# Both ConvFFN products of a two-layer encoder by Strassen's seven block products, in two phases with the activation's rows going through DRAM

## The chip, the cores and the metric

The kernel runs on one core of a Trainium2 chip. A core has TensorE (matrix products, out of SBUF into PSUM), VectorE, ScalarE, GpSimd (called Pool or POOL in the rows) and queues that start DMA transfers, here all by SyncE (SP). The metric is the device time of one execution in microseconds.

## The reference

The input x has 1024 positions of width 1024. Two layers follow each other; the first has a forgetting attention, the second a differential attention whose keys and values come from the first layer's end. After its attention each layer has a ConvFFN, which is what the change is about:

```python
def _conv_ffn(x, w_in, conv_w, conv_b, w_out):
    s = x.shape[1]
    u = x @ w_in                                   # 1024 -> 2 * 2816
    up = jnp.pad(u, ((0, 0), (CONV_WIDTH - 1, 0), (0, 0)))
    u = sum(conv_w[j] * up[:, j:j + s] for j in range(CONV_WIDTH)) + conv_b
    g, val = u[..., :D_FF], u[..., D_FF:]
    return (jax.nn.silu(g) * val) @ w_out          # 2816 -> 1024

x = _layer_norm(DN_ALPHA * x + mixer(x), ...)
x = _layer_norm(DN_ALPHA * x + _conv_ffn(x, ...), ...)
```

All values are float32.

## The kernel before

A float32 product is made of three products in a reduced format: each operand is split into a high part (a cast on ScalarE) and a low part (operand minus high part, a subtraction on VectorE or Pool, `split_w`, L173), and `mm3` (L186 to L197) sums high·high, high·low and low·high in PSUM. A matmul has a 128x128 weight block and 512 columns of the other operand.

x stands transposed in SBUF, as `xh` and `xl` for two halves of the positions. `x_from` (L235) makes it from a tile of 128 positions by eight transposes (`tps`), a cast and a subtraction for each half of the width.

`ffn` runs over 22 hidden tiles. `hidden(i)` loads the two weight tiles of a gate and a value tile, splits them, and makes `u` for all 1024 positions: 2 halves x 2 x 8 x 3 = 96 matmuls. Then come the convolution (one pass of ScalarE, L363, and two steps of VectorE, L365, for each half), Silu and the gate (L369), and the split into `hh` and `hl`. The activation stays in SBUF. `down` takes two hidden tiles at a time, 8 position tiles x 2 column halves x 2 x 3 = 96 matmuls into `dn`, and VectorE adds each result to `Y` (L398, L400). The down products of one pair of hidden tiles stand between the up products of the next. The last four hidden tiles are summed in `down_last`, where each position tile is normalised as its sum is done, and in layer 0 `tail_a` turns it into x again and starts the value projection (`vp`) of the next layer.

The start of `ffn` overlaps the attention's output projection: `op.tile(NT - 2)` and `steps` are its last two tiles of positions (`op` in the rows), and tiles that are done are turned into x between them. In the second layer the same function runs with other pools.

The order of each engine's instructions is set when the program is built, by a scheduler that starts from the order of the code and from priorities. At run time each engine takes its own queue in order, and waits where an operand isn't ready.

## Time and profile before

| what | value |
|---|---|
| median of 3 runs | 2674.91 us (2670.71 to 2676.68) |
| the profiled execution's own time | 2674.87 us |
| its span | 2673.1 us |
| mean granted clock of TensorE | 0.991 |
| TensorE / VectorE / ScalarE / Pool busy | 98% / 55% / 34% / 28% |
| DMA | 291.12 MB, mean 109 GB/s |

The span is the time from the first to the last instruction that the profile shows. A busy share counts matmuls as they overlap: a matmul row lasts about 0.39 us while the next one has begun 0.23 us after it. "PEclk" is the clock that the throttle granted, as a share of full speed. In rows, `out<-in` are the program's names; "idle before" is the time the engine stood still ahead of the instruction, with what ended it.

### The profile page before, as it was taken

How to read it: one execution, taken by the hardware profiler on the slowest of the kernel's cores; microseconds unless marked ns; L12 is line 12 of the kernel's file. 1: busy time of each engine (PE TensorE's matmuls, PEld its weight loads, DVE VectorE, ACT ScalarE, POOL GpSimd, SP SyncE). 2: the span in 40 equal slices, each digit the busy share in tenths (PEclk: the TensorE clock that was granted, in tenths of full speed). 3: DMA queues.
4: the chain of work that ended last, by engine and by line, in shares of the span. 5: the costliest groups of instructions: out<-in, count | busy, mean ns of one | idle time of the engine just before them, and what ended most of it. 6: DMA issues, size and time to landing. Idle time of an engine off the chain costs nothing. (4 is left out here: it accounts for less than half of the span.)

```text
span 2673.1 us, 35354 instructions
## 1 busy us (share of the span) xinstructions
PE 2619.5 (98%) x13576; PEld 2234.6 (84%) x13576; DVE 1457.0 (55%) x2742; ACT 917.7 (34%) x1544; POOL 760.8 (28%) x756
## 2 busy tenths in 40 slices
PE   8999999999999999999999999999999999999997
PEld 7989898777888888888888898988788888888886
DVE  5656656755444444444558685777544444444436
ACT  3544545523222222222235454553332222222221
POOL 3433334431111111111332545464411111111124
PEclk9999999999999999999999999989999999999999
DMA  7565646353111111111165546472521111111111
GB/s 251 170 191 163 209 147 192 127 191 122 48 48 48 48 49 54 48 48 48 56 199 165 174 125 205 129 237 76 204 92 50 53 48 48 48 48 48 48 40 63
DMA packets 136553, 291.12 MB, mean 109 GB/s; under 512 B 12464, under 2 KB 66736, under 8 KB 135360
## 3 DMA queue, kind: packets, MB, share of 16 engines
q1 hardware_dynamic: 136384, 288.86, 33.9%
q8 instruction: 107, 1.75, 0.3%
q14 instruction: 62, 0.51, 0.1%
HBM read 213.25 MB, written 75.56 MB: 108 GB/s over the span
## 5 line engine op out<-in xcount | busy, mean ns | idle before, releaser
L191 PE MATMUL u<-xh,whi 128*128 128x512 f32 x1408 | 547.9, 390 | 2.1 <-ACT xh L243 2.0
L191 PE MATMUL u<-xl,whi 128*128 128x512 f32 x1408 | 548.7, 390 | 0.1
L191 PE MATMUL u<-xh,wlo 128*128 128x512 f32 x1408 | 548.2, 389 | 0.0
L173 DVE TENSOR_TENSOR wlo<-raw,whi 128x1024 fp32r<-128x1024 f32 (+1 forms) x92 | 136.3, 1481 | 519.5 <-ACT whi L165 519.5
L191 PEld LDWEIGHTS u<-xh,whi 128*128 128x128 f32 x1408 | 264.0, 188 | 57.9 <-ACT xh L243 3.1
L191 PEld LDWEIGHTS u<-xl,whi 128*128 128x128 f32 x1408 | 264.3, 188 | 56.0 <-DVE xl L244 1.0
L191 PEld LDWEIGHTS u<-xh,wlo 128*128 128x128 f32 x1408 | 264.3, 188 | 54.8
L173 POOL TENSOR_TENSOR hl<-t,hh 128x1024 fp32r<-128x1024 f32 x42 | 100.7, 2397 | 641.6 <-ACT hh L165 641.6
L400 DVE TENSOR_TENSOR y<-y,dn 128x512 f32<-128x512 f32 x256 | 174.2, 685 | 173.7 <-PE dn L191 173.7
L191 PE MATMUL dn<-w2hi,hl 128*128 128x512 f32 x640 | 249.7, 390 | 0.0
L191 PE MATMUL dn<-w2lo,hh 128*128 128x512 f32 x640 | 249.7, 390 | 0.0
L191 PE MATMUL dn<-w2hi,hh 128*128 128x512 f32 x640 | 249.4, 390 | 0.0
L365 DVE SCALAR_TENSOR_TENSOR t<-u,cw,t 128x1023 f32<-128x1023 f32 (+1 forms) x176 | 224.9, 1278 | 40.6 <-ACT t L363 38.1
L173 POOL TENSOR_TENSOR w2lo<-raw,w2hi 128x1024 fp32r<-128x1024 f32 x40 | 96.1, 2402 | 479.3 <-ACT w2hi L165 448.6
L165 ACT CAST whi<-raw 128x1024 fp32r<-128x1024 f32 (+1 forms) x100 | 104.0, 1041 | 326.0 <-PE u L191 283.2
L191 PE MATMUL pj<-xh,whi 128*128 128x512 f32 x496 | 197.6, 398 | 2.0 <-DVE hl L645 1.9
L191 PE MATMUL pj<-xh,wlo 128*128 128x512 f32 x496 | 197.4, 398 | 0.0
L191 PE MATMUL pj<-xl,whi 128*128 128x512 f32 x496 | 197.1, 397 | 0.0
L501 DVE TENSOR_TENSOR tl<-tp,th 128x512 fp32r<-128x512 f32 (+1 forms) x240 | 149.9, 633 | 65.1 <-ACT th L500 60.2
L165 ACT CAST w2hi<-raw 128x1024 fp32r<-128x1024 f32 x40 | 42.0, 1051 | 384.7 <-PE dn L191 267.1
L500 ACT CAST th<-tp 128x512 fp32r<-128x512 f32 (+1 forms) x240 | 127.9, 543 | 119.5 <-PE tp L496 73.4
L684 POOL TENSOR_SCALAR pt<-pt,rr 128x128 f32<-128x128 f32 (+7 forms) x128 | 96.6, 761 | 221.7 <-DVE rr L683 179.9
(198 smaller groups left out, 5435.0 us busy)
## 6 DMA issues: line engine op xcount, KB each, us to landing
raw<-in_w_dram SPq DMA_DIRECT2D x132, 512.0 KB, 3.6
raw<-in_aqk_dram SPq DMA_DIRECT2D x16, 512.0 KB, 4.7
vd<-vt SPq DMA_DIRECT2D x32, 256.0 KB, 2.8
qd<-hl SPq DMA_DIRECT2D x32, 256.0 KB, 3.6
kd<-hl SPq DMA_DIRECT2D x32, 256.0 KB, 4.2
vv<-vd SPq DMA_DIRECT2D x16, 512.0 KB, 5.5
q<-qd SPq DMA_DIRECT2D x16, 512.0 KB, 4.6
ka<-kd SPq DMA_DIRECT2D x16, 512.0 KB, 6.1
```

What stands on the lines that cost most here:

```text
L165: nc.scalar.copy(out, in_)
L173: e.tensor_tensor(out, a, b, ALU.subtract)
L191: nc.tensor.matmul(ps, a, b, start=first and i == 0, stop=last and i == n - 1)
L365: nc.vector.scalar_tensor_tensor(t[:, j:], u[:, :S - j], cw[:, 2 - j, c:c + 1], t[:, j:], ALU.mult, ALU.add)
L400: nc.vector.tensor_tensor(Y[t][:, cc], Y[t][:, cc], o, ALU.add)
L500: nc.scalar.copy(th[:, :n], tp[:, :n])
L501: nc.vector.tensor_tensor(tl[:, :n], tp[:, :n], f32(th[:, :n]), ALU.subtract)
L684: nc.gpsimd.tensor_scalar(pt, pt, rr, 1.0, ALU.mult, ALU.mult)
```

## The change

The up product of a hidden pair and the down product are each cut into 2 x 2 blocks, and seven products of sums of blocks take the place of eight products of blocks.

Phase 1 (`hidden`, `w_parts`): the four weight blocks of a gate and a value tile (A11 to A22) give four sums S1 to S4; x gives four sums T1 to T4 and is kept as blocks B11, B21, B22. Seven products of 12 matmuls make the four results, three of which are summed in the PSUM bank `a`; ScalarE copies them into `ug` and `uv` and VectorE adds the others. Convolution and gate are as before. The gated row goes to DRAM (`h_d`); for each pair of hidden tiles Pool makes a sum of two halves (`s1_d`) and a difference of two weight halves (`t1_d`), which go to DRAM as well. The sums of x are made by `x_lo`, `x_hi` and `late`; those of three of the four position pairs take a way through DRAM (`xr_d`), as the pools have no room for them at first.

Phase 2: for each of seven products, eleven turns. A turn loads a pair of blocks of 128x512 from DRAM (`pair`), sums them where the product wants it, splits them together (`parted`: a ScalarE cast and a VectorE subtraction of 128x1024, into one of seven `opj` buffers) and runs 12 matmuls into four banks. Position tiles 4 to 7 are normalised during the seventh product, and tiles 0 to 3 after it.

The diff, cut to its core:

```diff
+        def x_lo(p, y, tags="TT"):
+
+            cs = slice(p * P, (p + 1) * P)
+            lows[p] = turned(y, tags)
...
+        def late(p, r, b22):
+
+            cs = slice(p * P, (p + 1) * P)
+            for h, src in (("T34", r), ("B22", b22)):
+                hi, lo = (w[..., cs] for w in X[h])
+                nc.scalar.copy(hi, src)
+                nc.vector.tensor_tensor(lo, src, f32(hi), ALU.subtract)
+
+        def x_hi(p, second, bounce):
+
+            cs = slice(p * P, (p + 1) * P)
+            (b11, b21), (b12, b22) = lows.pop(p), second
+            r, q = ((tmp if bounce else fp).tile([P, 2, 4, P], F32, name="xr", tag=tag, bufs=1 if bounce else 2)
+                    for tag in (("xr", "xq") if bounce else ("ug", "uv")))
+            nc.scalar.copy(r[:, 0], b12)
+            nc.vector.tensor_tensor(q[:, 0], b22, r[:, 0], ALU.subtract)
+            nc.vector.tensor_tensor(r[:, 0], r[:, 0], b11, ALU.subtract)
+            nc.vector.tensor_tensor(r[:, 1], b22, r[:, 0], ALU.subtract)
+            nc.vector.tensor_tensor(q[:, 1], b21, r[:, 1], ALU.subtract)
+            nc.scalar.copy(T12[0][..., cs], r)
+            nc.vector.tensor_tensor(T12[1][..., cs], r, f32(T12[0][..., cs]), ALU.subtract)
+            if bounce:
+                keep = tmp.tile([P, 512], F32, name="xb", tag="xb")
+                nc.scalar.copy(keep, b22.rearrange("p k s -> p (k s)"))
+                nc.sync.dma_start(out=xr_d[p][:, 0:2, :], in_=q.rearrange("p a k s -> p a (k s)"))
+                nc.sync.dma_start(out=xr_d[p][:, 2, :], in_=keep)
+            else:
+                late(p, q, b22)
...
+        x_lo(0, y[0])
+        x_hi(0, turned(y[1], "SS"), True)
         steps = op.tile(NT - 1)
-        for t in (4, 5):
-            plain(take(steps, 6))
-            x_from(Y[t], t)
+        plain(take(steps, 8))
+        x_lo(1, y[2])
+        y = [load_y(t) for t in (5, 2, 3)]
+        x_hi(1, turned(y[0], "SS"), True)
         plain(steps)
-        x_from(op.of(NT - 2), NT - 2, "TD")
...
+        x_lo(2, y[1])
+        x_hi(2, turned(op.of(NT - 2), "SS"), True)
+        x_lo(3, y[2], "SS")
...
+            split("A11", a11, "whi")
+            split("A12", a12, "wlo")
+            yield ops
+            s1 = both("S1", a21, a22, ALU.add)
+            s2 = both("S2", s1, a11, ALU.subtract)
+            split("S2", s2, "ws")
+            yield ops
+            split("S1", s1, "ws")
+            yield ops
+            split("S3", both("S3", a11, a21, ALU.subtract), "ws")
+            yield ops
+            split("S4", both("S4", a12, s2, ALU.subtract), "whi")
+            yield ops
+            split("A22", a22, "wlo")
+            yield ops
+
+        def product(ps, w, x, first=False):
...
+        def hidden(i, ops):
+
+            a = bank("S", "ua")
+            product(a, ops["A11"], X["B11"], first=True)
+            b = bank("D", "ub")
+            product(b, ops["A12"], X["B21"], first=True)
+            yield
+            ug = fp.tile([P, S], F32, name="ug", tag="ug", bufs=2)
+            uv = fp.tile([P, S], F32, name="uv", tag="uv", bufs=2)
+            with urgent():
+                nc.scalar.copy(ug[:, 0:512], a)
+                nc.vector.tensor_tensor(ug[:, 0:512], ug[:, 0:512], b, ALU.add)
+            product(a, ops["S2"], X["T2"])
+            with urgent():
+                nc.scalar.copy(ug[:, 512:S], a)
+            yield
+            c = bank("S", "uc")
+            product(c, ops["S1"], X["T1"], first=True)
+            with urgent():
+                nc.scalar.copy(uv[:, 512:S], c)
+            yield
+            product(a, ops["S3"], X["T3"])
+            with urgent():
+                nc.vector.tensor_tensor(uv[:, 512:S], uv[:, 512:S], a, ALU.add)
+            yield
+            product(c, ops["S4"], X["B22"])
+            with urgent():
+                nc.vector.tensor_tensor(ug[:, 512:S], ug[:, 512:S], c, ALU.add)
+            yield
+            product(a, ops["A22"], X["T4"])
+            with urgent():
+                nc.scalar.copy(uv[:, 0:512], a)
...
+                t = fp.tile([P, S], F32, name="tv" if half else "tg", tag="tv" if half else "tg", bufs=2 if half else 3)
+                nc.scalar.activation(t, u, AF.Identity, bias=cb[:, k:k + 1], scale=cw[:, 2, k:k + 1])
...
-            hi = fp.tile([P, S], F32R, name="hh", tag="hh", bufs=4)
-            lo = fp.tile([P, S], F32R, name="hl", tag="hl", bufs=4)
-            round_to("act", hi, ts[0])
-            sub("dve" if i == NH - 1 else "gps", lo, ts[0], f32(hi))
-            return hi, lo
...
+            nc.sync.dma_start(out=h_d[i], in_=ts[0])
+            made.append(ts[0])
+            if i % 2:
+                s1, m = made.pop(0), i // 2
+                nc.gpsimd.tensor_tensor(s1[:, 512:S], s1[:, 512:S], made.pop(0)[:, 512:S], ALU.add)
+                nc.sync.dma_start(out=s1_d[m], in_=s1[:, 512:S])
+                w = wpool.tile([P, D], F32, name="raw", tag="raw", bufs=2)
+                nc.sync.dma_start(out=w, in_=A["w2"][layer, 2 * m])
+                nc.gpsimd.tensor_tensor(w[:, 512:D], w[:, 512:D], w[:, 0:512], ALU.subtract)
+                nc.sync.dma_start(out=t1_d[m], in_=w[:, 512:D])
+            yield
...
+        parts = [w_parts(0), w_parts(1)]
+        todo = [hidden(i, next(g)) for i, g in enumerate(parts)]
+        for g in todo:
+            next(g)
+        y7 = turned(op.of(NT - 1), "TT")
+        fp = rest()
...
-        for n, c in enumerate(chunks):
-            hs = [hidden(c[0])]
-            if prev:
-                down(*prev)
-            hs += [hidden(i) for i in c[1:]]
-            prev = (c, hs, n == 0)
...
+        x_hi(3, y7, False)
+        for p in range(3):
+            r = fp.tile([P, 2, 4, P], F32, name="xr2", tag="ug", bufs=2)
+            b22 = fp.tile([P, 4, P], F32, name="xb2", tag="sr", bufs=3)
+            nc.sync.dma_start(out=r.rearrange("p a k s -> p a (k s)"), in_=xr_d[p][:, 0:2, :])
+            nc.sync.dma_start(out=b22.rearrange("p k s -> p (k s)"), in_=xr_d[p][:, 2, :])
+            late(p, r, b22)
+        plain(parts[0])
+        for i in range(NH):
+            g = todo[i]
+            if i >= 2:
+                next(g)
+            nxt = parts[i + 1] if i + 1 < len(parts) else None
+            if nxt is None and i + 1 < NH:
+                parts.append(w_parts(i + 1))
+                nxt = parts[-1]
+                todo.append(hidden(i + 1, next(nxt)))
+            for _ in range(6):
+                if next(g, 0) == 0:
+                    break
+                if nxt:
+                    next(nxt, None)
+            if nxt:
+                plain(nxt)
...
+        def pair(m, a, b):
+            tag = ("raw", "whi", "wlo", "whi", "wlo", "raw", "whi", "wlo")[ring[0] % 8]
+            ring[0] += 1
+            r = wpool.tile([P, 2, 512], F32, name="pr", tag=tag, bufs=2 if tag == "raw" else 3)
+            nc.sync.dma_start(out=r[:, 0], in_=src[a](m))
+            nc.sync.dma_start(out=r[:, 1], in_=src[b](m))
+            return r
...
+        def parted(*rs):
+            o = fp.tile([P, 2, 1088], F32R, name="opj", tag="opj", bufs=7)
+            if len(rs) == 1:
+                nc.scalar.copy(o[:, :, 0:512], rs[0])
+                nc.vector.tensor_tensor(o[:, :, 512:1024], rs[0], f32(o[:, :, 0:512]), ALU.subtract)
...
+        def turn(ps, o, m, first=False):
+            for t in range(4):
+                times(ps[t], o, t, first and m == 0, m == NM - 1)
...
+        As = [bank("S", "dna") for t in range(4)]
+        for m in range(NM):
+            turn(As, parted(pair(m, "A11", "B11")), m, first=True)
+        for t in range(4):
...
+            r5, r6 = pair(m, "S1", "T1"), pair(m, "A11", "B22")
+            nc.vector.tensor_tensor(s2[:, m], r5[:, 0], r6[:, 0], ALU.subtract)
+            nc.vector.tensor_tensor(t2[:, m], r6[:, 1], r5[:, 1], ALU.subtract)
+            turn(As, parted(s2[:, m], t2[:, m]), m)
+            turn(Cs, parted(r5), m, first=True)
...
+        def last(m):
+            r = pair(m, "A12", "B22")
+            nc.vector.tensor_tensor(r[:, 0], r[:, 0], s2[:, m], ALU.subtract)
+            return parted(r)
+
+        for t in range(4):
+            to_y(t + 4, lo_, As[t], True)
+            layer_norm(Y[t + 4], g_bc, b_bc, out(t + 4))
+        for m in range(NM - 4):
+            turn(Cs, last(m), m)
+            if m >= 2 and m < 6:
+                tail(m + 2, Y[m + 2], fp)
+        os = [last(m) for m in range(NM - 4, NM)]
+        for t in range(4):
+            for m, o in enumerate(os):
+                times(Cs[t], o, t, False, m == 3)
+
+            def add(h, t=t):
+                if h:
+                    to_y(t, hi_, Cs[t], False)
+
+            layer_norm(Y[t], g_bc, b_bc, out(t), t < 3, add)
+            tail(t, Y[t], fp)
...
-        if t == NT - 1:
-            plain(b_v(0, wv0, lambda: 0.0, range(0, 6)))
-            x_from(*pend.pop(0))
...
+        if t >= 4:
+            x_from(y, t, "SS")
+            if t == 6:
+                wv0.extend(b_v_weights(0))
+            return
...
+        if t == 3:
+            plain(b_v(0, wv0, lambda: 0.0, f, range(4, NT)))
+            x_from(*pend.pop(0), "TD")
```

Three places of the built order, each queue in its own order. First TensorE at the start of layer 0's ConvFFN, before: `tps` are the transposes of `x_from`, `yw` the last tile but one, `u` the first up product.

```order
L240 MATMUL tps<-ident_r,y_7195 128x128 [waits DMAHW3_49,DVE_49]
L240 MATMUL tps<-ident_r,y_7195 128x128 x3
L240 MATMUL tps<-ident_r,yw 128x128 x2
L191 MATMUL u<-xh_7198,whi 128x512 [waits Activation_49]
L191 MATMUL u<-xh_7198,whi 128x512
L240 MATMUL tps<-ident_r,y_7195 128x128 [waits DVE_49]
```

The first up matmuls stand between the transposes, and more transposes follow. The same place now, behind the A11 and A12 products of the first two hidden tiles: `yw` is the last tile, `ws` S2, `t12h` and `t12l` the parts of T2.

```order
L355 MATMUL tps<-ident_r,yw 128x128 [waits DVE_49,PE_49]
L355 MATMUL tps<-ident_r,yw 128x128 x3
L192 MATMUL ua<-t12h,ws 128x512 [waits Activation_49]
L192 MATMUL ua<-t12l,ws 128x512 [waits DVE_49]
L192 MATMUL ua<-t12h,ws 128x512 [waits DVE_49]
L192 MATMUL ua<-t12h,ws 128x512
L192 MATMUL ua<-t12l,ws 128x512
```

The S2·T2 product stands right behind the last tile's transposes; `ua<-b1h,whi` of the second hidden tile, with a wait for ScalarE, comes behind its 12 matmuls. On VectorE at the same place, now (the add that reads the last output matmul, L299, stands 20 rows further up; L373 is `late`, L425 and L420 are the sums and splits of `w_parts`):

```order
L373 TENSOR_TENSOR t34l<-xr_7634,t34h 128x8x128 [waits DMAHW4_49,DMAHW5_49,DMAHW0_49,Activation_49]
L373 TENSOR_TENSOR t34l<-xr,t34h 128x8x128 [waits Activation_49]
L373 TENSOR_TENSOR b22l<-xb_7635,b22h 128x4x128 [waits DMAHW6_49,Activation_49]
L373 TENSOR_TENSOR b22l<-xb_7643,b22h 128x4x128 [waits DMAHW7_49,Activation_49]
L373 TENSOR_TENSOR b22l<-xb_7651,b22h 128x4x128 [waits DMAHW0_49,Activation_49]
L425 TENSOR_TENSOR sr<-raw 128x512 [waits DVE_49]
L373 TENSOR_TENSOR t34l<-xr_7642,t34h 128x8x128 [waits DMAHW1_49,Activation_49]
L425 TENSOR_TENSOR sr<-sr,raw 128x512 [waits DVE_49]
L425 TENSOR_TENSOR sr<-raw 128x512
L373 TENSOR_TENSOR t34l<-xr_7650,t34h 128x8x128 [waits DMAHW2_49,Activation_49]
L459 TENSOR_TENSOR ug<-ug,ub 128x512 [waits Activation_49]
L420 TENSOR_TENSOR ws<-sr,ws 128x512 [waits Activation_49] x3
```

The low parts of T3, T4 and B22 stand ahead of the S2 low part (`ws<-sr,ws`), for which the product above waits. Second, VectorE in the first hidden tiles of layer 0, before, where the convolution of one tile (`t<-u`) meets the down products of two others:

```order
L173 TENSOR_TENSOR wlo<-raw,whi 128x1024 [waits DMAHW3_49,PE_49,Activation_49]
L398 SCALAR_TENSOR_TENSOR y_7192<-y_7192,dn 128x512 [waits PE_49]
L365 SCALAR_TENSOR_TENSOR t<-u,cw,t 128x1023 [waits Activation_49]
L398 SCALAR_TENSOR_TENSOR y_7192<-y_7192,dn 128x512 [waits PE_49]
L398 SCALAR_TENSOR_TENSOR y_7193<-y_7193,dn 128x512 [waits PE_49]
L365 SCALAR_TENSOR_TENSOR t<-u,cw,t 128x1022 [waits DVE_49]
```

The adds to `y` stand between the steps of a convolution. VectorE at the switch from phase 1 to phase 2 of layer 0, now:

```order
L471 TENSOR_TENSOR uv<-uv,ua 128x512 [waits PE_49,Activation_49]
L475 TENSOR_TENSOR ug<-ug,uc 128x512 [waits PE_49]
L486 SCALAR_TENSOR_TENSOR tg<-ug,cw,tg 128x1023 [waits DMAHW7_49,Activation_49]
L486 SCALAR_TENSOR_TENSOR tg<-ug,cw,tg 128x1022 [waits DVE_49]
L486 SCALAR_TENSOR_TENSOR tv<-uv,cw,tv 128x1023 [waits Activation_49]
L486 SCALAR_TENSOR_TENSOR tv<-uv,cw,tv 128x1022 [waits DVE_49]
L490 TENSOR_TENSOR tg<-tg,tv 128x1024 [waits DVE_49,Activation_49]
L576 TENSOR_TENSOR opj<-pr,opj 128x2x512 [waits DMAHW0_49,DMAHW1_49,PE_49,Activation_49]
L576 TENSOR_TENSOR opj<-pr,opj 128x2x512 [waits DMAHW3_49,DMAHW4_49,DMAHW2_49,Activation_49]
L576 TENSOR_TENSOR opj<-pr,opj 128x2x512 [waits DMAHW3_49,DMAHW5_49,DMAHW1_49,Activation_49]
```

All of the last hidden tile's convolution and gate stand ahead of the first split of phase 2 (`opj`). Third, TensorE at the end of layer 0's ConvFFN, before, from the last down matmuls:

```order
L191 MATMUL dn<-whi,hh 128x512
L191 MATMUL dn<-wlo,hh 128x512
L191 MATMUL dn<-whi,hl 128x512
L191 MATMUL vp<-whi,xh_11475 128x256 [waits Activation_49]
L191 MATMUL vp<-wlo,xh_11475 128x256
L191 MATMUL vp<-whi,xl_11476 128x256
```

The value projection `vp` follows the down product at once; the transposes of the last tiles stand between its later groups. The same place now (`y_10742` and `y_10743` are position tiles 2 and 3; those of tiles 0 and 1, which wait for Pool, stand right ahead):

```order
L245 MATMUL tps<-ident_r,y_10742 128x128 [waits DVE_49]
L245 MATMUL tps<-ident_r,y_10742 128x128 x3
L245 MATMUL tps<-ident_r,y_10743 128x128 [waits DVE_49]
L245 MATMUL tps<-ident_r,y_10743 128x128 x3
L192 MATMUL vp<-whi,x_12060 128x256 [waits DVE_49]
L192 MATMUL vp<-wlo,x_12060 128x256
```

The transposes of the tiles 0 to 3 stand ahead of the first `vp`.

## Rows read from the trace of the kernel before

**Rows 1.** The page: busy time by engine; then tenths busy of VectorE and granted clock by slice.

```profile
PE 2619.5 (98%) x13576; PEld 2234.6 (84%) x13576; DVE 1457.0 (55%) x2742; ACT 917.7 (34%) x1544; POOL 760.8 (28%) x756
...
DVE  5656656755444444444558685777544444444436
...
PEclk9999999999999999999999999989999999999999
```

**Rows 2.** Windows of 100 us in each ConvFFN: length, busy us (instructions) by engine, granted clock, DMA.

```profile
800.00:900.00 100.00, 100.00 (x443) 82.81 (x442) 45.39 (x49) 21.29 (x20) 13.63 (x6) 1.00 0.14 42
...
2100.00:2200.00 100.00, 100.00 (x442) 82.55 (x441) 43.13 (x41) 26.91 (x26) 14.38 (x6) 1.00 0.18 54
```

**Rows 3.** Groups by line and shape: busy us, mean ns of one, idle before, releaser.

```profile
L191 PE MATMUL u<-xh,whi 128*128 128x512 f32 x1408 | 547.9, 390 | 2.1 <-ACT xh L243 2.0
...
L400 DVE TENSOR_TENSOR y<-y,dn 128x512 f32<-128x512 f32 x256 | 174.2, 685 | 173.7 <-PE dn L191 173.7
...
L173 DVE TENSOR_TENSOR wlo<-raw,whi 128x1024 fp32r<-128x1024 f32 x90 | 135.1, 1501 | 517.8 <-ACT whi L165 517.8
...
L173 POOL TENSOR_TENSOR wlo<-raw,whi 128x1024 fp32r<-128x1024 f32 x47 | 113.8, 2423 | 27.9 <-ACT whi L165 25.8
...
L365 DVE SCALAR_TENSOR_TENSOR t<-u,cw,t 128x1023 f32<-128x1023 f32 x88 | 112.3, 1276 | 38.1 <-ACT t L363 38.1
...
L363 ACT ACTIVATE t<-u,cb,cw 128x1024 f32<-128x1024 f32 x88 | 105.9, 1204 | 5.2 <-PE u L191 5.2
...
L500 ACT CAST th<-tp 128x512 fp32r<-128x512 f32 x144 | 83.5, 585 | 75.1 <-PE tp L496 46.5 <-PE pv L693 21.2 <-PE pv L894 3.7
...
L369 DVE TENSOR_TENSOR t<-t 128x1024 f32<-128x1024 f32 x44 | 53.8, 1222 | 0.9
```

**Rows 4.** Timeline of TensorE at the start of layer 0's ConvFFN: start us, us, instruction, idle.

```profile
608.90 0.39 PE L191 MATMUL op<-wo_hi,ol 128*128 128x512 f32 x1
...
611.21 0.73 PE L191 MATMUL u<-xh,whi 128*128 128x512 f32 x2 [0.61 <-ACT xh L243]
612.52 0.66 PE L240 MATMUL tps<-ident_r,y 128*128 128x128 f32 x4 [0.58 <-DVE xl L244]
```

**Rows 5.** Line 173 on VectorE: ns min/median/max, first and last start.

```profile
L173 DVE TENSOR_TENSOR wlo<-raw,whi x92: 435/1226/2830, 4.8 to 2582.0; 128x1024 fp32r<-128x1024 f32 x90, 128x272 fp32r<-128x272 f32 x1, 128x544 fp32r<-128x544 f32 x1
...
L173 DVE TENSOR_TENSOR xl<-xraw,xh x16: 679/693/2200, 4.2 to 30.1; 128x512 fp32r<-128x512 f32 x16
```

**Rows 6.** DMA issues of the page: KB each, median us from issue to landing.

```profile
raw<-in_w_dram SPq DMA_DIRECT2D x132, 512.0 KB, 3.6
```

**Rows 7.** Timeline of TensorE behind layer 0's last down product.

```profile
1343.87 0.50 PE L191 MATMUL vp<-whi,xh 128*128 128x256 f32 x2 [2.11 <-ACT whi L165]
1344.86 0.63 PE L240 MATMUL tps<-ident_r,y 128*128 128x128 f32 x4 [0.49 <-DVE xl L244]
1346.65 1.09 PE L240 MATMUL tps<-ident_r,y 128*128 128x128 f32 x4 [1.17 <-DVE xl L244]
```

**Rows 8.** Windows near the start, behind layer 0's ConvFFN, and in the second attention.

```profile
8.00:10.00 2.00, 2.00 (x16) 2.00 (x16) 0.88 (x2) 0.42 (x2) 0.86 (x1) 1.00 1.08 380
...
1346.00:1348.00 2.00, 1.34 (x5) 1.02 (x6) 2.00 (x3) 0.33 (x2) 0.56 (x1) 0.62 0.00 0
1348.00:1350.00 2.00, 2.00 (x11) 2.00 (x11) 2.00 (x4) 0.37 (x1) 0.00 (x0) 0.52 0.55 96
...
1500.00:1600.00 100.00, 99.36 (x679) 90.94 (x678) 75.88 (x229) 55.96 (x133) 44.75 (x72) 1.00 0.50 154
...
1700.00:1800.00 100.00, 96.44 (x535) 82.79 (x534) 77.17 (x193) 52.15 (x115) 61.31 (x81) 0.93 0.60 193
```

**Rows 9.** Timeline of all engines at the program's end.

```profile
2657.97 0.39 PE L191 MATMUL dn<-whi,hl 128*128 128x512 f32 x1
...
2664.34 2.34 POOL L225 TENSOR_TENSOR y<-y,b_bc 128x1024 f32<-128x1024 f32 x1 [1.16 <-DVE y L224]
...
2669.26 0.99 SPq L231 DMA_DIRECT2D out_dram<-y  x2
```

More of the change, by code (lines that the diff above doesn't have):

```diff
@@ L184, in split_w, with mm3_steps @@
         return into
-    def mm3_steps(ps, pairs, every, cost, first=True, last=True):
+    def mm3_steps(ps, pairs, every, cost, first=True, last=True, joined=False):
         n = 3 * len(pairs)
@@ L190, in mm3_steps @@
             for a, b in ((lh, rh), (lh, rl), (ll, rh)):
-                nc.tensor.matmul(ps, a, b, start=first and i == 0, stop=last and i == n - 1)
+                nc.tensor.matmul(ps, a, b, start=first and i == 0, stop=last and i == n - 1,
+                                 skip_group_check=joined)
                 i += 1
@@ L237, in x_from @@
         for g in range(2):
-            ps = psum.tile([P, 4, P], F32, name="tps", tag=tags[g])
+            ps = bank(tags[g], "tps", [P, 4, P])
             for k in range(4):
@@ new lines, in ffn, with w_parts, split, both @@
+        x_lo(2, y[1])
+        x_hi(2, turned(op.of(NT - 2), "SS"), True)
+        x_lo(3, y[2], "SS")
+        def w_parts(i):
+            raw = [wpool.tile([P, D], F32, name="raw", tag="raw", bufs=2) for half in range(2)]
+            for half in range(2):
+                nc.sync.dma_start(out=raw[half], in_=A["w1"][layer, i + half * NH])
+            a11, a12, a21, a22 = (r[:, c:c + 512] for r in raw for c in (0, 512))
+            ops = {}
+            def split(name, src, tag):
+                w = (fp if tag == "ws" else wpool).tile([P, 2, 512], F32R, name=tag, tag=tag, bufs=4 if tag == "ws" else 3)
+                nc.scalar.copy(w[:, 0], src)
+                nc.vector.tensor_tensor(w[:, 1], src, f32(w[:, 0]), ALU.subtract)
+                ops[name] = w
+            def both(name, a, b, op):
+                r = fp.tile([P, 512], F32, name="sr", tag="sr", bufs=3)
+                nc.vector.tensor_tensor(r, a, b, op)
+                return r
[14 more added lines that the diff above has]
+            yield ops
@@ L443, in ffn @@
+        xp2, fp = then()
+        Y = [fp.tile([P, D], F32, name=f"y{t}") for t in range(NT)]
+        for t in range(NT):
+            nc.sync.dma_start(out=Y[t], in_=op.x_d[t])
+        g_bc = fp.tile([P, D], F32, name="g_bc")
+        b_bc = fp.tile([P, D], F32, name="b_bc")
         bc_row(g_bc, A["lnp"][4 * layer + 2])
         bc_row(b_bc, A["lnp"][4 * layer + 3])
-        if layer == 0:
-            new_x(xp)
-        for t, add in down_last(*prev[:2]):
-            layer_norm(Y[t], g_bc, b_bc, out(t), t < NT - 1, add)
-            tail(t, Y[t])
+        NM = NH // 2
@@ L990, in dense @@
                 if kind == "v":
-                    yield from b_v(i, w, clock, range(0 if n else 6, NT))
+                    yield from b_v(i, w, clock, pool, range(0, NT if n else 4))
                 else:
```

250 lines of the change are left out of this document (133 added, 117 removed).

## The prediction

> **What bounds the kernel now.** I read the busy shares first: TensorE works in 98% of the span, VectorE in 55%, ScalarE in 34% [rows 1]. The tenths by slice say where this holds: between the slices of 6 tenths there are two long valleys in which VectorE sits at 4, and those are the two ConvFFNs [rows 1]. Then the windows inside a ConvFFN: TensorE busy for 100.00 of 100 us, with 443 and 442 matmuls of 128x512, so one leaves every 0.2265 us (the durations near 0.39 overlap and are not the pace) [rows 2]. By the code a layer has 22 x 96 up matmuls and 1056 down, both layers 6336; at 0.2265 they are 1435 us, more than half the span. The up-projection's group waited 2.1 us in the whole program [rows 3]. So a matmul taken away there is worth its full pace, as long as the other engines still feed TensorE; and the question of this change is what it asks of VectorE, which had half its time free.
>
> **What the change removes.** Seven block products replace eight: 84 matmuls for 96 per hidden tile, 924 for 1056 per down projection. Per layer that is 22 x 12 + 132 = 396, and the built program has 792 matmuls fewer (13514 to 12722 TensorE instructions, transposes alike). 792 x 0.2265 = 179.4 us off. VectorE goes from 2552 to 3174 instructions and ScalarE from 1290 to 1788; Pool loses 60. That is covered or not stage by stage.
>
> **Start of each ConvFFN.** Before, TensorE goes from the last attention-output matmul over a few transposes to the first up matmul in 2.3 us, and idles 0.61 and 0.58 there [rows 4], since an x tile needs one ScalarE copy and one VectorE subtraction. Now four sums of x blocks, two splits and the bounced tiles stand ahead. Between the add that reads the last output matmul (L299) and the first `ws` subtraction, for which S2·T2 waits, lie 31 instructions on VectorE's queue, the last of them in the third order piece. I priced them: 21 of 128x512 at 0.69, a small one, 9 of 128x1024 at 1.23 to 1.27 [rows 3, 5], 26 us, with the normalisation's Pool steps and ScalarE copies they wait for about 31 us. TensorE has 32 transposes (some 4.7 us) and 24 of the four early products' matmuls (5.4 us) to put beside it. So it idles about 21 us. Behind S2·T2 it waits once more: the second hidden tile's A11 can be loaded only when the first one's S4 has been read, because the raw ring holds two tiles; a load takes 3.6 us to land [rows 6], so +4. The clock is added: at the end of layer 0, after an idle of 2.11 us and one of 1.17, the granted clock stood at 0.62 and 0.52 for two windows of 2 us, the lower of its two levels, 1.2 of 2.4 GHz, for most of them [rows 7, 8]; (0.38 + 0.48) x 2 = 1.7 us per such gap, here 2.4 for one and a half. 21 + 4 + 2.4 - 1.2 = 26 per layer, **+52**. Ends: nothing gained over before, 0, if VectorE had done most of it while TensorE still ran the last output tile; 40 per layer if each ScalarE copy shows.
>
> **Phase 1.** Per hidden tile VectorE has 6 weight low parts and 4 weight sums of 128x512 at 0.693, 3 sums from PSUM at 0.685, 4 convolution steps at 1.28 and the gate at 1.22 [rows 3, 5]: 4.2 + 2.8 + 2.1 + 5.1 + 1.2 = 15.3 us, against 84 x 0.2265 = 19.0 on TensorE, 81%. ScalarE has 6 casts and 4 copies of 128x512 at 0.585, two passes of 128x1024 at 1.20 and Silu, taken like them: 9.5 [rows 3]. So VectorE stays under TensorE, but it has to turn round results in order, seven times per hidden tile. The dependencies have room: the A11 and A12 products of the next tile stand between the results of this one. The nearest rows for such a load are two attention windows with VectorE at 76 and 77%: TensorE at 99.36 and 96.44 [rows 8], a mean loss of 2.1%. At 81% I take 3% of 22 x 19.0 = 418 us: 12.6 per layer, **+25**. Ends: 0, and 2.1 us per hidden tile (the fourth rival). The weights and the writes of h, S1 and T1 are some 2.1 MB per 19 us, 110 GB/s, and hide behind the matmuls: an attention window moved 193 [rows 8].
>
> **Switch to phase 2.** The first down product needs the last hidden tiles: the fifth order piece has VectorE do four convolution steps, the gate and then the first `opj` subtraction in a row. From the last up matmul: copy 0.6, pass 1.2, two convolution steps 2.5, gate 1.2, cast and subtraction about 1.2 beyond what overlaps: 7 us, with the clock about 8; before, `dn` and the next up-projection alternated and no such point was. Twice: **+16** (0 to 12 each; at the upper end a round trip of h through DRAM shows).
>
> **Phase 2.** A turn is 12 matmuls, 2.72 us, for two loads of 256 KB: 0.524 MB per 2.72 us = 193 GB/s. The window from 1700 moved just that at a DMA share of 0.60, and a window of 2 us near the start 380 GB/s [rows 8]. VectorE: 77 subtractions of 128x1024 at 1.226, 66 sums of 128x512 and 28 adds from PSUM at 0.685, 158 us, and the normalisation of four tiles about 17: 175 of 924 x 0.2265 = 209. Seven `opj` buffers give TensorE up to 19 us of lead over its bursts. I take 3 per layer for the change of products, **+6** (0 to 28: the third rival's price). The subtraction's duration is the median of 1.226, not the mean of 1.5: the long ones, up to 2.83, are those in which Pool ran a subtraction of its own of 2.42 [rows 3, 5], and Pool has none of those here.
>
> **Ends.** Layer 0: before, the value projection `vp` followed the last `dn` at once and took the wait of four tiles' normalisation beside it; the idle there is 2.11 + 0.49 + 1.17 [rows 7]. Now the transposes of the tiles 0 to 3 stand ahead of the first `vp` (last two pieces), and behind VectorE's queue of tiles 4 to 7: 21 us of parts, 17 of normalisation, 8 of x low parts and adds in a product of 30 us. TensorE idles about 18 in place of 3.8: **+15** (0 to 25). Layer 1: the last `dn` at 2657.97, the last store's issue at 2669.26, the span's end 3.8 later [rows 9]; four tiles instead of one are left to normalise then, with Pool's add of 2.34 ahead of the last tile's root on the same queue: **+3** (-3 to +8).
>
> **Sum.** The profiled execution took 2674.87 us (span 2673.1), 0.04 from the median of the runs, so no correction: 2674.9 - 179.4 + 52 + 25 + 16 + 6 + 15 + 3 = 2612.5. **I predict 2612 us.**
>
> A rule on the other side: the granted clock fell in the two windows named and was 0.93 in a window with TensorE at 96.44% busy [rows 8]. The Trainium skill, TensorE: Matmul & The Clock Gate, in its section on HAM oscillation, says that matmul groups broken up again and again by waits start at the lower clock each time. By it the new waits of phase 1 would each cost clock beside their idle; the trace agrees for those two rows, and no row shows it for gaps as short as phase 1 should have. The sum by that rule is the second rival's.
>
> **Rivals.**
> 1. VectorE's start is covered. If the x blocks are done while the last output tile still multiplies, the start costs 10 per layer in place of 26, and phase 1 loses 1% as 1500:1600 did [rows 8]: 2612 - 32 - 17 = 2563. For it: in the order, tiles 0 to 2 are done early. Against it: the 31 instructions are behind the last output add.
> 2. Half clock in phase 1. With the 0.93 of the window from 1700 instead of 3%: 837 / 0.93 - 837 = 63 for 25: 2650. For it that window; against it, phase 1 works all on 512 columns, and its waits are on copies already issued.
> 3. Loads bound phase 2. If the pairs arrive at 170 GB/s, between the 154 and 193 of the two attention windows [rows 8], a turn lasts 3.08 and 154 turns cost 55: 2667. For it: rows of 2 KB, two loads per turn and ring slots that come free late. Against it: 380 GB/s.
> 4. VectorE bounds phase 1: slower. Ten times per hidden tile a VectorE step waits for a ScalarE copy made just before it (six splits, four copies or passes). Before, that wait was 518 us of idle on VectorE and cost nothing, as it was idle anyway [rows 3]. If each copy of 0.585 shows, 15.3 + 5.9 = 21.2 per tile: 2.1 over TensorE, times 44 = 94 in place of 25, 2681; it decides from 21.0 per tile on: 2.0 us x 44 = 88 is the forecast's 25 and its gain of 62. Against it: the order puts splits a product ahead.
> 5. That the products are not fewer, or run longer: excluded by the count, except if a matmul accumulating into a bank that ScalarE has just read were slower than 0.2265; at 0.238 (62 us over 5544 matmuls) the gain is gone. Then 2670 to 2680.
>
> **Chances.** Forecast 0.55 (its own range 2590 to 2637), covered start 0.14, half clock 0.10, loads 0.08, VectorE bound 0.10, no gain 0.03. About 0.2% is what a measurement of this kernel can tell from no change. Faster: 0.55 + 0.14 + 0.10 + 0.08 = 0.87; slower: 0.10; within: 0.03. The range 2555 to 2660 leaves out the last of these, part of the loads' case and the best of the covered start: about 2 in 10.
>
> **What would show it.** The saving: 12 matmuls fewer per hidden tile at a spacing still near 0.2265. The start: one idle of about 20 us on TensorE before `ua<-t12h,ws`, ended by VectorE. Phase 1: VectorE at 75 to 85% and TensorE at 96 to 98% in windows; VectorE at 95% there is rival 4, a clock below 0.95 rival 2. The switch: some 7 us before `dna<-opj`. Phase 2: idle on TensorE ended by DMA is rival 3. Layer 0's end: idle at `tps` ended by Pool and VectorE. The forecast is wrong if phase 1 takes more than 20 us per hidden tile or less than 19.1.

## The result, and the profile after

The changed kernel takes 2616.6 us (median of 4 runs, 2612.1 to 2618.3) against 2675.1 for the kernel before, a ratio of 0.9781 with a 95% interval of 0.9764 to 0.9798. The forecast was 2612. The span of the profiled execution fell from 2673.1 to 2614.4, by 58.7 us, where 792 matmuls at their pace are 179.4: about a third of the saving arrived.

The page of the changed kernel, to be held against [rows 1]: busy time by engine, then the slices of TensorE, VectorE and the granted clock.

```profile
PE 2467.5 (94%) x12784; PEld 2103.4 (80%) x12784; DVE 1887.1 (72%) x3364; ACT 1173.3 (45%) x2042; POOL 615.8 (24%) x696
...
PE   8999999997999999999899999989979999999997
...
DVE  5656555767787788687838686877688887776778
...
PEclk9999999998999999999999999998989999999998
```

TensorE lost 152 us of busy time, and its share fell from 98 to 94%. The valleys of VectorE at 4 tenths are now at 6 to 8.

The windows of the ConvFFNs: the start, phase 1, the switch, phase 2 and the end in layer 0, then phase 1 and phase 2 in layer 1 (length, busy us by engine, granted clock, DMA share, GB/s).

```profile
605.00:655.00 50.00, 32.84 (x142) 25.37 (x140) 38.64 (x55) 22.85 (x37) 0.88 (x4) 0.80 0.41 146
655.00:1071.00 416.00, 402.43 (x1765) 329.99 (x1763) 330.61 (x394) 196.38 (x293) 39.11 (x21) 1.00 0.36 114
1071.00:1110.00 39.00, 37.91 (x160) 31.26 (x161) 25.11 (x24) 20.06 (x20) 2.19 (x1) 0.94 0.94 350
1110.00:1275.00 165.00, 160.49 (x701) 132.16 (x700) 130.48 (x169) 61.18 (x69) 5.25 (x6) 0.99 0.56 186
1275.00:1350.00 75.00, 59.25 (x364) 53.65 (x363) 46.46 (x66) 22.44 (x36) 21.82 (x19) 0.86 0.38 130
...
1965.00:2372.00 407.00, 393.20 (x1706) 322.44 (x1705) 314.12 (x376) 186.14 (x279) 41.22 (x21) 0.99 0.35 112
...
2400.00:2580.00 180.00, 173.58 (x753) 142.85 (x752) 141.27 (x181) 70.49 (x77) 4.68 (x6) 0.98 0.55 188
```

Where [rows 2] had TensorE busy throughout, the windows of phase 1 leave 13.6 and 13.8 us idle by layer, with VectorE at 79 and 77%. (The 5.7 us of the switch, before the first `dna` at 1072.1 and 2375.9, lie partly in them; phase 1's own are 9.0 and 12.0.) The first 50 us leave 17.2, the end of layer 0 15.8. Phase 1 does not lose evenly. Its first and its last full 100 us in layer 0:

```profile
655.00:755.00 100.00, 100.00 (x442) 82.49 (x441) 80.89 (x100) 49.00 (x74) 11.30 (x5) 1.00 0.35 113
...
955.00:1055.00 100.00, 95.10 (x416) 77.33 (x415) 80.95 (x94) 47.21 (x71) 9.74 (x6) 1.00 0.38 117
```

VectorE is at 81% in both, TensorE at 100.00% in one and at 95.10% in the other. The list of TensorE's waits names the losses (us in total, times, longest):

```profile
PE ua L192 <- ACT ws L419: 28.0, 2, 14.3
PE ua L192 <- ACT ug L462: 19.1, 12, 3.0
PE tps L245 <- POOL y L227: 13.2, 2, 10.3
PE dna L192 <- ACT opj L575: 12.6, 3, 5.7
PE dna L192 <- DVE y L596: 7.3, 2, 4.0
```

These are, in order, the start (once a layer), phase 1, layer 0's end, the switch (5.7 a layer), and the changes of product in phase 2.

### The profile page after: what moved, and what is told of

It is laid out like the page before. It is cut to its first block, busy times and chain, and to the rows that moved or that the text cites. A ratio compares the mean times of both kernels' runs of the same rounds, so it can differ in the third digit from the quotient of the medians.

```text
span 2614.4 us, 35909 instructions
## 1 busy us (share of the span) xinstructions
PE 2467.5 (94%) x12784; PEld 2103.4 (80%) x12784; DVE 1887.1 (72%) x3364; ACT 1173.3 (45%) x2042; POOL 615.8 (24%) x696
## 5 line engine op out<-in xcount | busy, mean ns | idle before, releaser
L192 PE MATMUL pj<-x,whi 128*128 128x512 f32 x992 | 322.9, 398 | 1.0 <-DVE hl L851 1.0
L192 PE MATMUL dna<-opj 128*128 128x512 f32 x1056 | 252.4, 398 | 22.3 <-ACT opj L575 12.6
L192 PEld LDWEIGHTS dna<-opj 128*128 128x128 f32 x1056 | 203.2, 193 | 67.7 <-ACT opj L575 13.8
L192 PEld LDWEIGHTS pj<-x,whi 128*128 128x128 f32 x992 | 184.5, 189 | 36.3 <-DVE hl L851 1.5
L192 PE MATMUL pj<-x,wlo 128*128 128x512 f32 x496 | 197.6, 398 | 0.0
L192 PE MATMUL vp<-whi,x 128*128 128x256 f32 (+1 forms) x960 | 195.3, 290 | 1.8 <-DVE vt L811 1.1
L576 DVE TENSOR_TENSOR opj<-pr,opj 128x1024 fp32r<-128x1024 f32 x132 | 159.3, 1218 | 35.7 <-ACT opj L575 34.0
L192 PE MATMUL dnc<-opj 128*128 128x512 f32 x792 | 184.6, 389 | 0.0
L192 PE MATMUL op<-wo,oh 128*128 128x512 f32 x512 | 160.6, 395 | 4.1 <-DVE y L301 3.1
L192 PEld LDWEIGHTS vp<-whi,x 128*128 128x128 f32 x960 | 155.0, 191 | 5.6 <-issue 1.3
L192 PE MATMUL ua<-t12h,ws 128*128 128x512 f32 x352 | 119.8, 402 | 30.1 <-ACT ws L419 28.0
```

Of the source, the lines that this page charges most:

```text
L192: nc.tensor.matmul(ps, a, b, start=first and i == 0, stop=last and i == n - 1, skip_group_check=joined)
L576: nc.vector.tensor_tensor(o[:, :, 512:1024], rs[0], f32(o[:, :, 0:512]), ALU.subtract)
```

## The experiments

Each kernel is the changed one with one edit. Its time stands beside 2616.6. The kernel before was timed again beside each group of them, at 2675.0 to 2675.7 us, so the times can be compared.

**A buffer of its own for T1.** In phase 1 of layer 1, the chain that ended last in the changed kernel runs not along TensorE but round the two `raw` buffers. A piece of it (start, us, what), one pair of hidden tiles long:

```profile
2117.88 1.62 POOL raw L499
2119.52 2.13 DMA t1d<-raw
2121.67 4.97 DMA raw<-in_w_dram
...
2127.39 1.29 DVE sr L425 x2
...
2129.37 1.25 ACT tg L484
2130.64 1.28 DVE tg L486
...
2139.20 4.56 DMA raw<-in_w_dram
...
2152.50 1.30 DVE wlo L420 x2
2153.82 3.45 DMA raw<-in_w_dram
2157.48 1.54 POOL raw L499
2159.03 2.02 DMA t1d<-raw
2161.07 5.52 DMA raw<-in_w_dram
```

One round, from load to load (2121.67 to 2161.07), takes 39.4 us; the 168 matmuls of a pair take 38.1. The T1 difference of every second hidden tile holds a `raw` buffer for a load, Pool's subtraction and a store, some 7 us in which no weight can be loaded into it.

```diff
-                w = wpool.tile([P, D], F32, name="raw", tag="raw", bufs=2)
-                nc.sync.dma_start(out=w, in_=A["w2"][layer, 2 * m])
+                for n in range(4):
+                    w = fp.tile([P, 2, 128], F32, name="w2t", tag="w2t", bufs=1)
...
```

> The T1 difference of phase 1 gets a small buffer of its own (four chunks of 128 columns) instead of one of the two `raw` buffers. Theory (the ring of two raw buffers, shared by the weight loads and the T1 difference, is a chain that is slower than TensorE): TensorE's waits on `ug` in phase 1, 9.0 and 10.2 us by layer, go to under 2 each, TensorE is at 99.5% or more between 655 and 1071 us instead of 96.7%, and the time falls by 15 to 27 us, to about 2595. Rival (VectorE's load of about 80% is the cause, it comes late with its results): nothing in VectorE's work changes, the waits stay, the time stays within 4 us of 2616.6.

2687.5 us, 71 slower. Theory and rival were both wrong on the time, but the windows of layer 0 hold an answer and a new cost:

```profile
655.00:755.00 100.00, 84.75 (x363) 69.01 (x362) 63.80 (x82) 41.36 (x62) 18.76 (x18) 0.93 0.32 99
755.00:855.00 100.00, 82.64 (x327) 65.31 (x326) 59.82 (x76) 37.29 (x56) 17.46 (x20) 0.91 0.34 105
...
955.00:1055.00 100.00, 100.00 (x443) 82.86 (x442) 80.51 (x100) 49.90 (x75) 5.46 (x3) 1.00 0.27 92
```

All T1 pieces ran in the first 250 us, and while they did TensorE was at 83 to 85%. Once they were done it was at 100.00% with VectorE at 80.51%. What they cost is read from SP's queue in that stretch (start of issue, us):

```profile
681.75 0.55 SPq L500 DMA_DIRECT2D w2t<-in_w_dram  x1
686.61 0.33 SPq L502 DMA_DIRECT2D t1d<-w2t  x1
686.99 0.42 SPq L491 DMA_DIRECT2D hd<-tg  x1
688.15 0.55 SPq L500 DMA_DIRECT2D w2t<-in_w_dram  x1
692.48 0.33 SPq L502 DMA_DIRECT2D t1d<-w2t  x1
```

Load and store alternate, each waiting for the other, and everything else issued by SP stands between them: after the two weight loads that began to be issued at 680.63, the next one came at 707.00.

**Without T1.** The load and the subtraction are gone, and the S1 half is stored in T1's place, so this kernel leaves out part of the computation and serves for its time alone.

```diff
-                w = wpool.tile([P, D], F32, name="raw", tag="raw", bufs=2)
-                nc.sync.dma_start(out=w, in_=A["w2"][layer, 2 * m])
-                nc.gpsimd.tensor_tensor(w[:, 512:D], w[:, 512:D], w[:, 0:512], ALU.subtract)
-                nc.sync.dma_start(out=t1_d[m], in_=w[:, 512:D])
+                nc.sync.dma_start(out=t1_d[m], in_=s1[:, 512:S])
```

> Leaves out the T1 difference of phase 1: its weight load through the raw ring and Pool's subtraction are gone, and the S1 half is stored in its place. The four-chunk buffer of the earlier run put 88 serial load-store pairs on SP's queue and so did not answer the question; this does. Theory (the raw ring with T1 in it): TensorE at 99.5% or more from 655 us to the switch, the stretch from the last output matmul to the first down product falls from 463 and 470 us to about 450 and 455, the time by 15 to 27 us. Rival (VectorE at 80% cannot turn results round in time): TensorE stays at 96 to 98%, the time within 5 us of 2616.6.

2589.4 us, 27.2 faster, as the theory had it; from the last output matmul to the first down product 452.1 and 452.5 us for 463.1 and 469.9. Phase 1:

```profile
655.00:755.00 100.00, 100.00 (x443) 82.81 (x442) 83.90 (x107) 51.35 (x75) 3.88 (x2) 1.00 0.29 98
```

The windows up to 1055 read 100.00 alike, with VectorE at 75 to 84%, in the one shown higher than in the changed kernel (83.90 for 80.89). So VectorE's share alone is no bound, and what costs phase 1 its time is T1. T1 brought three things: the hold on a `raw` buffer, a load of 512 KB and Pool's subtraction for each pair. The chain above picks the first, and in the changed kernel TensorE was at 100.00% in its first 100 us with all three present. That fits a ring that starts with a lead: T1's stores in layer 0 follow each other after 37.3 to 37.8 us at first, as the matmuls do, and after 39.0 to 41.3 from the fourth pair on. A run that takes the three apart was not made.

**One product twice.** The same from the other side: more matmuls in phase 1.

```diff
-            product(a, ops["A11"], X["B11"], first=True)
+            for _ in range(2):
+                product(a, ops["A11"], X["B11"], first=True)
```

> The A11 product runs twice per hidden tile, the second time over the first: 12 matmuls more, 528 in all, 119.6 us at 0.2265. Theory (phase 1 is paced in its second half by the raw ring, whose length has no matmul in it): the 27 us of waits there disappear behind the extra matmuls, and the time rises by 90 to 105 us. Rival (the waits are handshakes after each product and stay beside the extra work): it rises by 117 to 125 us.

2706.9 us, 90.3 more; all windows from 655 to 1055 at 100.00% TensorE, such as the last:

```profile
955.00:1055.00 100.00, 100.00 (x443) 82.81 (x442) 74.11 (x89) 42.58 (x62) 8.48 (x5) 1.00 0.27 93
```

T1 and its ring are as before here; a pair now has 192 matmuls, 43.5 us, more than the 39.4 of the round. 528 matmuls at 0.2265 are 119.6, so 29 us of them were hidden: the 21 us of idle in phase 1 (the expectation's 27 had counted 6 of the switch's), and some of the clock, which stood at 0.99 over the 407 us of layer 1. It lies at the theory's edge and far from the rival's 117.

**The weight sums on Pool.**

```diff
-                nc.vector.tensor_tensor(r, a, b, op)
+                nc.gpsimd.tensor_tensor(r, a, b, op)
```

> The four weight sums S1 to S4 per hidden tile run on Pool instead of VectorE. Rival (VectorE's load costs phase 1 its 3%): VectorE falls from 79 to about 65% there, the waits of phase 1 go, the time falls by 15 to 25 us. Theory (the chain from the raw loads over the sums to the raw buffers): a sum takes 1.3 to 1.6 us on Pool for 0.69 on VectorE, so each hidden tile's chain grows by 2 to 4 us; the time rises by 20 to 150 us, to 2640 or more, although VectorE has less to do.

2608.8 us, 8 faster. Both expectations were wrong: less work for VectorE did not bring the 15 to 25 us back, and longer sums in the chain did not cost 20. TensorE's idle time in phase 1 was 8.3 and 7.3 us for 9.0 and 12.0, with VectorE at 75%. Where the 8 us come from is not shown. A shorter round of the ring is one candidate: VectorE's steps (`sr`, `tg`, `wlo`) are links of its chain. But the waits on `ug`, 11.4 us here for 19.1, came to 14.0 in the run `vpfirst` below, whose edit is not in phase 1, and to 24.8 and 23.3 in two runs below that have the changed kernel's own order.

**T1 ahead of the gate.** The four T1 lines stand before the A22 product.

> The T1 load and difference stand ahead of the gate and Pool's S1 sum in the code, still in the raw ring. Theory (the raw buffer of T1 is held until Pool has done the S1 sum, which waits for the gate): the buffer comes free some 5 us earlier, the waits of phase 1 halve, the time falls by 5 to 15 us. Rival (the hold is the load and the store on SP's queue): the order on Pool changes nothing, within 4 us.

2616.4 us, no change. The edit moved nothing: in the trace the instructions of every engine stand in the same order as in the changed kernel, so the run cannot decide between theory and rival. The changed kernel's own trace answers the theory. Pool makes the T1 difference (`raw`) of a pair before that pair's S1 sum (`tg`), as the scheduler had already put it:

```profile
669.38 1.83 POOL L499 TENSOR_TENSOR raw<-raw 128x512 f32<-128x512 f32 x1 [55.06 <-DMA raw<-in_w_dram]
687.93 2.22 POOL L495 TENSOR_TENSOR tg<-tg 128x512 f32<-128x512 f32 x1 [16.72 <-DVE tg L490]
```

So it is not the wait for the S1 sum that holds the buffer. The run is worth something as a second execution of the same order: the waits on `ug` summed to 24.8 us for 19.1, so such a sum is uncertain by several us.

**The first hidden tile's sums ahead of the bounced x tiles.**

```diff
+        plain(parts[0])
         for p in range(3):
             r = fp.tile([P, 2, 4, P], F32, name="xr2", tag="ug", bufs=2)
...
             late(p, r, b22)
-        plain(parts[0])
```

> At the start of each ConvFFN the weight sums and splits of the first hidden tile stand ahead of the bounced x tiles. Theory (TensorE's 14 us of idle ahead of S2·T2 is VectorE's queue): the wait shrinks by the six late low parts and their waits, 5 to 8 us, part of which comes back as a wait before S3·T3, whose operands are now last; 2 to 7 us per layer are left, the time falls by 4 to 14 us. Rival (the wait is for the weight load or the x tiles' way through DRAM, whatever the order): the time stays within 3 us.

2594.3 us, 22 faster, where 4 to 14 were expected. From the last output matmul to the first down product the layers take 459.7 and 458.8 us for 463.1 and 469.9, 14.5 less. The other 8 lie in stretches that the edit doesn't touch. Part of the 14.5 may be phase 1's own scatter; a cleaner value comes from the last runs below, where phase 1 has no idle: with this edit the same stretch is 5.8 and 5.6 us shorter (444.8 and 443.8 in the three together for 450.6 and 449.4 with T1 in phase 2 alone). So about 11 of the 22 are shown to be this edit's. TensorE's idle before S2·T2 in the changed kernel, then the only long one of this kernel in the same stretch, and its window:

```profile
634.29 0.79 PE L192 MATMUL ua<-t12h,ws 128*128 128x512 f32 x1 [14.26 <-ACT ws L419]
636.57 1.22 PE L192 MATMUL ua<-t12h,ws 128*128 128x512 f32 x2 [1.07 <-DVE ws L420]
642.41 0.80 PE L192 MATMUL ua<-b1h,whi 128*128 128x512 f32 x1 [1.21 <-ACT whi L419]
```

```profile
632.32 0.79 PE L192 MATMUL ua<-b1h,whi 128*128 128x512 f32 x1 [11.56 <-ACT whi L419]
```

```profile
605.00:655.00 50.00, 37.81 (x177) 30.68 (x176) 45.72 (x65) 27.30 (x44) 1.45 (x5) 0.90 0.46 156
```

The order decides, but most of the wait moved: the idle of these 50 us fell from 17.2 to 12.2, the granted clock rose from 0.80 to 0.90, and what is left stands before the next hidden tile's A11 product, not before S3·T3 as expected.

**The value projection ahead of the transposes** at layer 0's end, in the banks that the transposes of tiles 4 to 7 used.

```diff
...
         pend.append((y, t))
-        if t:
-            x_from(*pend.pop(0), "TD")
         if t == 3:
-            plain(b_v(0, wv0, lambda: 0.0, f, range(4, NT)))
-            x_from(*pend.pop(0), "TD")
+            plain(b_v(0, wv0, lambda: 0.0, f, range(4, NT), "S"))
+            for p in pend:
+                x_from(*p, "TD")
```

> At the end of layer 0's ConvFFN the value projection of the positions 512 to 1023 stands ahead of the transposes of the tiles 0 to 3, with its results in the banks that the transposes of the tiles 4 to 7 used. Theory (the 15 us of idle there come from the order, transposes that wait for Pool and VectorE ahead of work that is ready): the projection's 13 us hide the normalisation, the idle falls from 15 to 2 to 6 us, the time falls by 8 to 13 us. Rival (VectorE is the bound of that stage, so that the projection's own operands come late): the first `vp` waits as the transposes did, the time stays within 4 us.

2603.3 us, 13 faster by the medians; the four runs spread from 2596.9 to 2617.9, and the interval of the ratio (0.9703 to 0.9769) just overlaps the changed kernel's. In the changed kernel TensorE's waits at that end are the 13.2 us on Pool in the list above and 2.5 more. Here:

```profile
PE tps L245 <- DVE x L249: 5.3, 2, 3.6
PE vp L192 <- DVE x L249: 1.8, 1, 1.8
PE tps L245 <- POOL y L227: 0.8, 1, 0.8
```

15.7 us of waits became 7.9, more than the 2 to 6 expected; from the first down product to the next layer's first masked score it is 7.0 us shorter, so half of the 13 is from this place. The rest lies mostly in phase 1, where the code is the same.

**High priority for the adds to Y.** `to_y` inside `with urgent()`.

> The adds of finished down products to Y get the scheduler's high priority. Theory (between products TensorE waits because these adds stand behind splits of later turns in VectorE's queue): the waits of dna on them, 3.3, 4.0 and 2.4 us, go to 1 or less each and the time falls by 4 to 9 us. Rival (the wait is the adds' own length, four of 0.69 us with the bank): within 3 us.

2619.6 us, no gain. At the change from the fifth to the sixth product the adds stand behind the same split as before (3.86 us of wait for 3.34). Again every engine's order is the changed kernel's: the edit moved nothing, so the theory on that wait was not tested.

**T1 in phase 2.** All of the computation, with T1's two blocks loaded in the ring of eight and subtracted there by Pool.

```diff
-            r5, r6 = pair(m, "S1", "T1"), pair(m, "A11", "B22")
+            r5, r11, r6 = pair(m, "S1", "B12"), pair(m, "B11", None), pair(m, "A11", "B22")
+            nc.gpsimd.tensor_tensor(r5[:, 1], r5[:, 1], r11[:, 0], ALU.subtract)
```

> The T1 difference moves from phase 1 to phase 2: its two weight blocks are loaded there in the ring of eight and Pool subtracts in place; nothing of it goes through the raw ring or DRAM. The whole computation is done. Theory (raw ring with T1): phase 1 as in the run without T1, TensorE at 99.5% or more; phase 2 has 22 loads of 256 KB more than before less 22 of the T1 rows and some longer VectorE steps beside Pool, 0 to 5 us; the time falls by 20 to 27 us, to about 2592. Rival (the load of phase 2 has no room: VectorE at 84%, loads of 193 GB/s): phase 2's third and fourth product grow by 10 us per layer, and the gain shrinks to under 8 us.

2599.0 us, 17.6 faster, between the theory's 20 to 27 and the rival's under 8. Phase 1 came out as the theory had it (450.6 and 449.4 us to the first down product, 12.5 and 20.5 less). Phase 2 and what follows it lost 10.5 and 7.3, the size that the rival had, but not in the third and fourth product, which ran without a gap on TensorE. The fifth product's loads come late. In layer 0 VectorE's waits for them sum to little more than in the changed kernel (12.5 us for 10.3), but one of them is 6.9 us long where the longest was 2.2, and TensorE waits 8.3 us for VectorE's add behind them.

```profile
DVE pr L619 <- DMA pr<-hd: 12.5, 7, 6.9
```

```profile
1190.04 32.34 PE L192 MATMUL dna<-opj 128*128 128x512 f32 x132 [8.30 <-DVE y L591]
```

**The three together, and with the sums on Pool.**

> T1 in phase 2, the first hidden tile's weight sums ahead of the bounced x tiles, and the value projection ahead of the transposes of the tiles 0 to 3, together. Theory (three separate places, losses that add up): 27 + 13 + 11 to 22 us off, 2552 to 2568. Rival (the raw ring gave slack back that the other two edits now lose, or the gain of the second was phase 1's): 2572 to 2590.

> The same with the four weight sums on Pool. Theory (with the ring free of T1, TensorE is the bound of phase 1 and VectorE's 80% costs nothing): within 4 us of the run without it, or slower at the start of the ConvFFNs, where the sums are on TensorE's path and cost 0.6 to 0.9 us more each. Rival (VectorE's load still costs phase 1, which is why the sums on Pool alone brought 8 us): 6 to 12 us faster than that run.

2575.8 us (ratio to the kernel before 0.9622, 0.9606 to 0.9638) and 2571.9 us (0.9614, 0.9599 to 0.9629). The value projection stands a little earlier in these two than in its own run, ahead of tile 0. The first is 41 faster than the changed kernel, where theory had 49 to 65 and the rival 27 to 45. It falls in the rival's range for a third reason: to the first down product the layers take 18.3 and 26.1 us less than in the changed kernel, but from there to the last one 11.7 and 4.1 more, with the two waits that T1 in phase 2 had brought before:

```profile
PE dna L192 <- DVE y L591: 18.1, 2, 9.3
```

The sums on Pool bring 4 more, with intervals that overlap: within the 4 us of the theory, and not the rival's 6 to 12. Both kernels beat the one before and the changed one.

## Why the prediction was right, and where its reason was not

The sum held stage by stage to within 7.5 us, with errors of both signs that in part made each other good (markers in both traces: last output matmul, last down matmul, first masked score, end of the span).

| term | predicted, us | measured, us |
|---|---|---|
| matmuls removed | -179.4 | -179.4 (792 fewer by the two pages; 442 in the 100 us from 655, the pace of [rows 2]) |
| ConvFFN, layer 0: start 26, phase 1 12.5, switch 8, phase 2 3 | +49.5 | +42.6 (729.6 to 682.5) |
| ConvFFN, layer 1, the same | +49.5 | +51.1 (729.2 to 690.6) |
| end of layer 0 | +15 | +16.7 |
| end of layer 1 | +3 | +2.7 |
| second attention | 0 | +7.5 |

- **Start.** S2·T2 began 25.3 us after the last output matmul (609.03 to 634.29), not 31. VectorE's queue was the cause, as said: it was busy for 30.1 of the 33 us from 605 to 638, and the 26 us of instructions were priced right; the 5 us added for ScalarE and Pool were mostly not there. The second wait was 1.21 instead of 4, since the load ran beside S2·T2, which took some 6 us at the low clock. The granted clock was 0.80 over these 50 us. (One and a half gaps at 1.7 us are 2.6, not the 2.4 of the prediction.) In the run without T1, where phase 1 lost nothing, 452.1 us less 418.6 for 1848 matmuls and some 4 for 32 transposes leave 29 to 30 us a layer for start and switch, where 34 were predicted: the start was sized some 5 us too high.
- **Phase 1.** 12.6 was predicted a layer, and 9.0 and 12.0 us of idle measured (11.0 and 17.4 us of time, by the run without T1), but the reason was wrong. The step "at 81% I take 3%" took VectorE's load for the cause, from attention windows with a similar load [rows 8]. The runs show a ring of two weight buffers with T1 in it: without T1 TensorE is at 100.00% with VectorE at 84%. The prediction had used that ring for the start only; it did not follow it round once and hold that against 38.1 us per pair. That the number is near is chance.
- **Rival 4** (a VectorE bound) had the same wrong premise. Rival 2's lower clock showed in phase 1 only in small: 1.00 in layer 0, where no wait is over 2.2 us, and 0.99 in layer 1, where the two longest waits, 2.91 us before 2218.17 and 2.95 before 2342.61, each have a stretch at the lower level beside them:

```profile
2219.00:2222.00 3.00, 3.00 (x9) 2.33 (x8) 3.00 (x5) 0.64 (x2) 0.46 (x1) 0.50 0.35 141
2342.00:2348.00 6.00, 5.39 (x13) 4.24 (x14) 5.96 (x6) 2.52 (x6) 2.67 (x2) 0.50 0.32 98
```

  At half speed TensorE loses about 4 us in these 9. The rule of the Trainium skill, TensorE: Matmul & The Clock Gate, in its section on HAM oscillation, thus fits the start and the switch (0.80 and 0.94) and these two waits, and none of the other waits of phase 1.
- **Switch.** 5.7 us of idle a layer and a granted clock of 0.94 over the next 39 us: 8 as predicted.
- **Phase 2.** 4.5 and 6.4 us of idle, at the changes of product, for 3. The split of 128x1024 took its undisturbed time, as [rows 5] had suggested:

```profile
L576 DVE TENSOR_TENSOR opj<-pr,opj x132: 1171/1218/1227, 1072.2 to 2585.1; 128x1024 fp32r<-128x1024 f32 x132
```

  Rival 3 (the loads) did not show in the changed kernel, but there was little room for more: in the run with T1 in phase 2, one load of 256 KB more in each second turn of two products, with Pool's subtraction behind it, cost about 9 us a layer.
- **Ends.** The transposes waited 10.3 and 3.0 us for Pool at layer 0's end, as the order of the rows said. At the end of layer 1 Pool's add of 2.34 us did stand ahead of the last tile's root:

```profile
2606.99 2.34 POOL L227 TENSOR_TENSOR y<-y,b_bc 128x1024 f32<-128x1024 f32 x1
2609.28 0.55 POOL L216 TENSOR_TENSOR rs<-rs,mhalf 128x1 f32<-128x1 f32 x1
2609.86 1.42 DVE L231 SCALAR_TENSOR_TENSOR y<-y,rs,b_bc 128x512 f32<-128x512 f32 x2 [3.01 <-POOL rs L216]
```

- **What was not forecast.** The second attention, to layer 1's last output matmul, took 7.5 us more. 3.5 of them lie between its first and last masked score, where the kernels here, with the same code, took 420.5 to 427.6 us. The other 4.0 come after that score (102.5 us for 98.5) and show in every variant (102.0 to 102.5). Most of these are moved work: 14 output matmuls and 7 transposes that stood ahead of that score before, and 8 transposes of the ConvFFN's start. What did grow is TensorE's idle time between the scores, 13.2 us for 7.1, although it has less to do there. What lengthened it was not tried.

## What to carry to other kernels

Count the arithmetic that a faster algorithm saves, and then every chain that it leaves: here two thirds of 179 us were lost again, mostly to the start, the buffer ring and the switch of each layer and to the end of the first one, and start, switch and end were read from the order of instructions before a run. A load share of an engine does not say whether it costs time; follow a buffer round once (load, last reader, store, next load) and hold that against the matmuls of the same round. If a value has to be made for later, don't make it in the buffers that feed the bound engine, and don't issue its loads and stores alternately on the queue that feeds it. And see in the trace whether an edit moved the instructions that it was to move: two of the edits here left every engine's order as it was.

## What the runs showed that was not expected

- In the run `own`, a load and a store that wait for each other on SP's queue held up all that was issued behind them: with 88 such pairs the kernel lost 71 us, where the run without T1 gained 27.
- In the run without T1, TensorE was busy for 100.00% of windows of 100 us with VectorE at up to 84%, ScalarE at 51% and seven hand-overs per 19 us.
- Adding 528 matmuls cost 90.3 us, 0.171 each, where the pace is 0.2265: part of them ran in time that TensorE had spent waiting for the ring.
- One program order, run three times with a profile, had 19.1, 24.8 and 23.3 us of waits on `ug`: a difference of a few us between two traces of phase 1 says nothing of an edit.
